# A new order of mixer units and small weights, a fourth product in an accumulator bank, and late low inputs, in a two-layer SSD and DeltaNet trunk

## The chip, the cores and the metric

The kernel runs on one core of one Trainium2 chip. The metric is the device time of one execution in microseconds. The kernel before has a median of 1545.27 us over three runs.

## The reference

The input is one sequence of 256 tokens with 1024 features in float32. Two layers follow, each a half-step SwiGLU feed-forward block, a token mixer and a second feed-forward block. The mixer has a Mamba-2 branch (SSD, 32 heads in four groups) and a gated DeltaNet branch (eight heads) on the same normalised input:

```
for l in range(DEPTH):
    h = h + 0.5 * swiglu(rms_norm(h, ffn1_norm[l]), ffn1_w_in[l], ffn1_w_out[l])
    u = rms_norm(h, mix_norm[l])
    (z_s, xbc, dt_s, qkv, z_d, b_d, a_d, gate_s, gate_d) = jnp.split(u @ w_in[l], split_points, axis=-1)
    y_s = mamba2_branch(z_s, xbc, dt_s, ssm_conv_w[l], ...)
    y_d = deltanet_branch(qkv, z_d, b_d, a_d, dn_conv_w[l], ...)
    merged = (jax.nn.sigmoid(gate_s) * (y_s @ ssm_w_branch[l])
              + jax.nn.sigmoid(gate_d) * (y_d @ dn_w_branch[l]))
    h = h + merged @ w_out[l]
    h = h + 0.5 * swiglu(rms_norm(h, ffn2_norm[l]), ffn2_w_in[l], ffn2_w_out[l])
return rms_norm(h, final_norm)
```

In the Mamba-2 branch, x, B and C go through a causal convolution of four taps and SiLU. Per group and chunk of 128 tokens, the products of C and B are weighted by a decay, applied to x times dt, and joined by the state of the chunk before.

## The kernel before, in words

**Products and weights.** Each float32 product is made of three matmuls: an operand is split into a high part (hi) and the rest (lo), and hi·hi, hi·lo and lo·hi are summed in PSUM. Weights come from HBM as 512 KB forms in one stream on SP's queue into five raw buffers (wraw); ACT writes the high part (whi, L68), DVE the low part (wlo, L71), into five pairs of split buffers. A split pair is rewritten once its last product is done. Activations that enter a product are split in the same way: bh by ACT and bl by DVE for a branch's input, mh and ml for the merged input of the output product.

**PSUM.** Four accumulator banks (`accb`) and four banks for transposes and small products (`trb`) are given out in turn: an allocation gets the bank of the fourth one before it, and its first matmul waits until that tile's last reader is done.

**The mixer's order.** The list ORDER names units, and a scheduler turns the code so written into one instruction stream per engine. The names used here:

- x*gi*: the weights' product for half of group g of x (48 matmuls into an accumulator bank `xs`), then per 128 channels a convolution: one step of ACT and three of DVE (`ca`, of 255, 254 and 253 columns), and SiLU on ACT (`xsT`). The last `ca` steps free the bank.
- D*g*: the decay of group g: a 1 MB DMA of `rdram` into `dc`, then on DVE a subtraction and a minimum with zero, an exponential on ACT, and a product with `cbt` on DVE.
- S*g*: transposes of `xsT` into two banks `xsb`, and on DVE `xD`, `xdt` and `xe` from them.
- T*g*: the products `ydb` (two banks) and `yob`, five sums on DVE, then the sums of squares (`jk`, `sss`), a reciprocal root on POOL (`srr`) and two scalings of `yz` on ACT.
- o: the transposes `oT` of the DeltaNet output's first head pair, `og` on DVE, then its split into bh and bl. y: the same for SSD (`yT`).
- N: the DeltaNet branch's product with its weights, 96 matmuls of 128x512 into four accumulator banks `b` (two halves of the tokens, two of the columns), with the other three `oT` in between.
- g*sni*: a quarter of a gate's product, with `tg` as its result.

Products of C and B (`cbb`, one bank per group, `ssd_pre`) come earlier, at the unit P. Each reads as `cbt` once DVE has masked it. `vb` on DVE is the DeltaNet's last correction, out of a `trb` bank (`ob`).

**The start of a mixer.** Its small weights are loaded on SP: lp (per channel), the next norm's nw, rp (per head, for all rows) and wsr (the 48 columns of dt, b and a), whose high part wsc ACT makes. The small product psm goes through smT and the transposes pst to dt; `ea` and `z` are exponentials on ACT.

**The output product.** `close` calls `out_chunks` for the merged input, k = 0 and 1 first as one group of weights.

Of the kernel before, what the change touches and what calls it, by code (L numbers as in the profile page):

```python
# [7 lines left out]
F32 = mybir.dt.float32  # L8
# [37 lines left out]
ORDER = """  # L46
z20 s z10 z11 s z21 s M k1 k0 q1 k2 k3 K1 K0 q3 q0 K3 K2 v0 q2 I Q0 I Q3 I z30 v1 z31 Q2 v2 V0 I v3
V1 I V3 I Q1 V2 d0 R R R b3 R b2 b0 R b1 R d2 R x00 R d1 x01 R d3 R R P R g100 g101 D0 S0 x10 T0 D1
x11 g110 g111 S1 x20 T1 o x21 N D2 y S2 D3 x30 x31 T2 g000 g010 g001 S3 g011 T3
""".split()  # L50


# [1 line left out]
def trunk_kernel(ctx, tc, x, wst, wsm, norms, lpar, rpar, cst, out):  # L54
# [279 lines left out]
    def mm3(ps, lh, ll, rh, rl, start, stop):  # L334
        PE.matmul(ps, lh, rh, start=start, stop=False)  # L335
        PE.matmul(ps, lh, rl, start=False, stop=False)  # L336
        return PE.matmul(ps, ll, rh, start=False, stop=stop)  # L337
# [55 lines left out]
                        cut and a == 0 and kt == 1,  # L393
                    )

    def out_chunks(ps, stat, ks, last, group=1, split=False, first=None):

        for g0 in range(0, len(ks), group):
            kk = ks[g0 : g0 + group]
            ws = [(k, take()) for k in kk]  # L400
            for t in range(2):
                order = [(k, n) for n in range(2) for k in range(len(kk))]
                if t == 1 and not split:
                    m = len(kk) - 2 if len(kk) == NSPL else len(kk)
                    order = [(k, n) for k in range(m) for n in range(2)]
                    order += [(k, n) for n in range(2) for k in range(m, len(kk))]
                order = [(k, n, 0, 512) for k, n in order]
                if t == 1 and split:
                    order = [o for o in order if o[1] == 0]
                    order += [(k, 1, c, c + 256) for c in (0, 256) for k in range(len(kk))]  # L410
                state["sums"] = []
                for k, n, c0, c1 in order:
                    k, (wh, wl) = ws[k]
                    sh, sl = stat(k, t)
                    c = slice(n * 512 + c0, n * 512 + c1)
                    begin = k == 0 if first is None else first and t == n == 1
                    bank = ps[t][n][:, c0:c1]
                    if c0:
                        begin, bank = k == kk[0], ps[2][:, 0:256]
                    ins = mm3(bank, sh, sl, wh[:, c], wl[:, c], begin, k == last)  # L420
                    state["sums"].append(ins)

    def residual(po, nw):
        def add(t):
# [11 lines left out]

    def close(po, stat, n_k, nw):

        out_chunks(po, stat, list(range(2)), n_k - 1, group=2)
        out_chunks(po, stat, list(range(2, n_k - NSPL)), n_k - 1)  # L440
        state["hold"] = True
        out_chunks(po, stat, list(range(n_k - NSPL, n_k)), n_k - 1, group=NSPL, split=nw is None)
        return residual(po, nw)
# [148 lines left out]

    def mixer(l, nxt):
        with tc.issue_after(state["last"].ins):
            lp = cpool.tile([P, LPW], F32, tag="lp", name="lp")
            nc.sync.dma_start(lp[:], lpar[l])
            rp = cpool.tile([P, RPW], F32, tag="rp", name="rp")
            nc.sync.dma_start(rp[:], rpar[l].partition_broadcast(P))
            wsr = s2.tile([P, KT, 48], F32, tag="s2", name="wsr")
            nc.sync.dma_start(wsr[:], wsm[l])  # L600
        snw = lp[:, 240:256]
        dnw = lp[:, 256:257]
        alog = rp[:, 40:80]
# [47 lines left out]
        def scalars():  # L651
            psm = trb("psm")
            for kt in range(KT):
                both = wsc[:, kt].rearrange("p o c -> p (o c)")
                if kt < KT - 1:
                    PE.matmul(psm[0:96, 0:S], both, uTh[:, kt, :], start=kt == 0, stop=False)
                PE.matmul(psm[0:48, 0:S], wsc[:, kt, 0], uTl[:, kt, :], start=False, stop=False)
                if kt == KT - 1:
                    PE.matmul(psm[0:96, 0:S], both, uTh[:, kt, :], start=False, stop=True)
            smT = s2.tile([96, S], F32, tag="s2", name="smT")  # L660
            act(smT[:], psm[0:96, 0:S])
            pst = trb("pst")
            for t in range(2):
                PE.transpose(pst[:, t * 96 : (t + 1) * 96], smT[:, t * P : (t + 1) * P], ident[0:96, 0:96])
            pv2 = pst[:, 0:192].rearrange("p (t o c) -> p t o c", t=2, o=2)
            pvs = small([P, 2, 48], "pvs", 1)
            pv = pvs[:]
            act(pv, pv2[:, :, 1])
            tt(pv, pv2[:, :, 0], pv, ALU.add)
            scr = s2.tile([P, 5, 2, 40], F32, tag="s2", name="scr")  # L670
            xb, ax, z, s_, q_ = (scr[:, i] for i in range(5))
            tt(xb, pv[:, :, 0:40], rp[:, None, 0:40].to_broadcast([P, 2, 40]), ALU.add)
            act(dq[:, :, 8:16], pv[:, :, 40:48], AF.Tanh, scale=0.5)
            ts(dq[:, :, 8:16], dq[:, :, 8:16], 0.5, ALU.mult, 0.5, ALU.add)
            ea = small([P, 40], "ea", 1)
            with tc.issue_after(state["input"][0].ins):
                act(ea[:], alog, AF.Exp)
            stt(ax, xb, -1.0, xb, ALU.mult, ALU.max)
            act(z, ax, AF.Exp, scale=-1.0)
            ts(s_, z, 2.0, ALU.add)  # L680
            V.reciprocal(out=s_, in_=s_)
            tt(s_, s_, z, ALU.mult)
            tt(q_, s_, s_, ALU.mult)
            ts(z, q_, 1.0 / 15.0, ALU.mult)
            for d_ in (13.0, 11.0, 9.0, 7.0, 5.0, 3.0):
                stt(z, z, 1.0 / d_, q_, ALU.add, ALU.mult)
            stt(z, z, 1.0, s_, ALU.add, ALU.mult)
            ts(ax, xb, 0.0, ALU.max)
            stt(sp[:], z, 2.0, ax, ALU.mult, ALU.add)
            stt(la[:], sp[:], -1.0, ea[:, None, :].to_broadcast([P, 2, 40]), ALU.mult, ALU.mult)  # L690
            yield
            psr = trb("psr")
            for t in range(2):
                PE.matmul(psr[0:40, t * 256 : (t + 1) * 256], la[:, t, :], UU, start=True, stop=True)
            pr = psr[:].rearrange("p (t c) -> p t c", t=2)
            V.tensor_copy(rows[0:32], pr[0:32, :, 0:P])
            V.tensor_copy(rows[32:40], pr[32:40, :, P : 2 * P])
            nc.sync.dma_start(rdram[:], rows[:].rearrange("p t c -> p (t c)"))
            pac = trb("pac")
            for t in range(2):  # L700
                PE.transpose(pac[:, t * 40 : (t + 1) * 40], rows[:, t, :], ident[0:40, 0:40])
            V.tensor_copy(ac[:], pac[:, 0:80].rearrange("p (t c) -> p t c", t=2))
            V.tensor_copy(dq[:, :, 0:8], ac[:, :, 32:40])
            yield
            psp = trb("psp")
            for c in range(4):
                PE.matmul(psp[:, c * 16 : (c + 1) * 16], SEL[c % 2], dq[:, c // 2, :], start=True, stop=True)
            for a in range(2):
                V.tensor_copy(
                    pq[64 * a : 64 * a + 64].rearrange("p k h c -> p c k h"),  # L710
                    psp[64 * a : 64 * a + 64, 0:64].rearrange("p (c k h a) -> p c k h a", c=4, k=2, h=4)[:, :, :, :, a],
                )
# [325 lines left out]
        def ssd_pre():  # L1038
            BT, CT = late["BC"][:, 0:4], late["BC"][:, 4:8]
            cbt = slots.tile([P, 3 * GS, P], F32, tag="sF", name="cbt")  # L1040
            late["cbx"] = cbx = cbt[:, 2 * GS :]
            late["cbm"] = cbm = cbt[:, : 2 * GS].rearrange("p (g t) l -> p g t l", g=GS)
            for g in range(GS):
                cbb = trb("cbb")
                PE.matmul(cbb[:, 0 : 2 * P], BT[:, g, 0:P], CT[:, g, :], start=True, stop=True)
                PE.matmul(cbb[:, 2 * P : 3 * P], BT[:, g, P : 2 * P], CT[:, g, P : 2 * P], start=True, stop=True)
                tt(
                    cbm[:, g],
                    cbb[:].rearrange("p (t o l) -> p t o l", t=2, o=2)[:, :, 0, :],
                    U[:, None, :].to_broadcast([P, 2, P]),  # L1050
                    ALU.mult,
                )
                act(cbx[:, g], cbb[:, P : 2 * P])
            yield
# [226 lines left out]
    norm_first(nw0)  # L1281
    for l in range(DEPTH):
        ffn(norm_vec(3 * l + 1))
        mixer(l, norm_vec(3 * l + 2))
        add = ffn(norm_vec(3 * l + 3) if l + 1 < DEPTH else None)
    nw = norm_vec(3 * DEPTH)
    for t in range(2):
# [151 lines left out]
```

## Time and profile before

| | us |
|---|---|
| median of three runs | 1545.27 (1545.19 to 1546.01) |
| the profiled execution, its own time | 1543.84 |
| its span, first to last instruction | 1542.1 |
| PE busy | 1525.1 |
| DVE busy | 1229.8 |
| ACT busy | 949.8 |
| POOL busy | 82.6 |

PE is TensorE, DVE VectorE, ACT ScalarE, POOL GpSimd, SP SyncE. A row of the timeline gives a start, a busy time, the engine, the line, the operation with output and inputs, the shape and the count, and in brackets the idle time ahead of it with what ended it. Successive instructions overlap by a little, so the time that one costs in a queue is read from start to start. The list of waits gives for each line and releaser the total in us, the number and the longest. A window gives for a stretch of time the busy us of PE, of PE's weight loads, DVE, ACT and POOL, each with its count, then the granted clock, the DMA share and GB/s.

### The profile page before, as it was taken

The page shows a single profiled execution, that of the slowest core. Times are in us where ns is not written, and L with a number is a line of the kernel's source. Part 1 is how long each engine was busy: PE and PEld are TensorE (multiplying, and loading weights), DVE is VectorE, ACT ScalarE, POOL GpSimd, SP SyncE. Part 2 cuts the span into 40 slices and gives each one's busy share as a digit, 9 for nine tenths or more (in the row PEclk, how much of TensorE's full clock was granted, in tenths as well). Part 3 has the DMA queues.
Part 4 walks back from the last instruction along what each step waited for, and adds up shares of the span by engine and source line. Part 5 has one row for each costly group of instructions (what it writes and reads, how often), then busy time and mean ns, then how long its engine had stood idle before and what let it go on. Part 6 is the DMA issues. An engine that isn't in the chain of part 4 may idle for free.

```text
span 1542.1 us, 29082 instructions
## 1 busy us (share of the span) xinstructions
PE 1525.1 (99%) x11473; PEld 1385.3 (90%) x11473; DVE 1229.8 (80%) x1859; ACT 949.8 (62%) x1536; POOL 82.6 (5%) x92
## 2 busy tenths in 40 slices
PE   8999999999999999999999999999999999999998
PEld 7999879999988888999899998899998888899997
DVE  5878768967899766789778887689579996678886
ACT  5656667766665645566555566776756666455565
POOL 0000010000000000000100012010000000000010
PEclk9999999999999999999999999999999999999999
DMA  7687765553565556577866687566346555556775
GB/s 272 187 266 227 232 223 174 183 164 112 180 209 172 157 174 191 184 252 217 264 221 227 204 254 238 182 196 186 117 137 204 180 167 187 175 179 191 250 241 156
DMA packets 98831, 305.73 MB, mean 198 GB/s; under 512 B 22837, under 2 KB 23813, under 8 KB 97670
## 3 DMA queue, kind: packets, MB, share of 16 engines
q1 hardware_dynamic: 93796, 290.95, 57.1%
q0 software_dynamic: 4608, 12.58, 5.0%
q8 instruction: 90, 1.47, 0.4%
q14 instruction: 47, 0.39, 0.1%
q10 hardware_dynamic: 290, 0.33, 0.1%
HBM read 297.72 MB, written 1.92 MB: 194 GB/s over the span
## 4 chain that ended last, share of the span: by engine, by line
PE 90%; DVE 3%; ACT 3%; DMA 2%; issue 1%; POOL 0%; SPq 0%; POOLq 0%; ACTq 0%; DVEq 0%
PE fc L346 10%; PE fc L340 9%; PE fc L345 9%; PE t L366 9%; PE o L337 4%; PE o L336 4%; PE o L335 4%; PE f L366 3%; PE b L337 3%; PE b L335 3%; PE b L336 3%; PE p L336 2%; PE p L335 2%; PE p L337 2%; PE xs L340 1%; PE xs L345 1%
## 5 line engine op out<-in xcount | busy, mean ns | idle before, releaser
L71 DVE TENSOR_TENSOR wlo<-wraw,whi 128x1024 fp32r<-128x1024 f32 x488 | 592.2, 1222 | 189.9 <-ACT whi L68 175.4
L68 ACT ACTIVATE whi<-wraw 128x1024 fp32r<-128x1024 f32 x488 | 511.4, 1059 | 266.8 <-PE fc L345 87.3
L346 PE MATMUL fc<-uW,wlo 128*128 128x256 f32 x1280 | 354.9, 277 | 0.0
L340 PE MATMUL fc<-uW,whi 128*128 128x256 f32 x1280 | 354.1, 277 | 0.0
L345 PE MATMUL fc<-uW,whi 128*128 128x256 f32 x1260 | 348.3, 276 | 0.0
L340 PEld LDWEIGHTS fc<-uW,whi 128*128 128x128 f32 x1280 | 240.5, 188 | 0.8
L346 PEld LDWEIGHTS fc<-uW,wlo 128*128 128x128 f32 x1280 | 240.5, 188 | 0.0
L345 PEld LDWEIGHTS fc<-uW,whi 128*128 128x128 f32 x1260 | 236.5, 188 | 0.8
L366 PE MATMUL t<-whi,uW 128*128 128x512 f32 x512 | 165.4, 397 | 0.0
L366 PEld LDWEIGHTS t<-whi,uW 128*128 128x128 f32 x512 | 95.9, 188 | 21.6 <-issue 1.3
L68 ACT ACTIVATE whi<-wsum 128x1024 fp32r<-128x1024 f32 x64 | 68.0, 1062 | 58.7 <-PE fc L345 32.3
L366 PE MATMUL t<-wlo,uW 128*128 128x512 f32 x256 | 100.1, 392 | 0.0
L71 DVE TENSOR_TENSOR wlo<-wsum,whi 128x1024 fp32r<-128x1024 f32 x64 | 78.2, 1222 | 8.3 <-ACT whi L68 5.9
L335 PE MATMUL b<-whi,bh 128*128 128x512 f32 x192 | 76.1, 398 | 0.3 <-ACT bh L68 0.2
L336 PE MATMUL b<-wlo,bh 128*128 128x512 f32 x192 | 75.0, 390 | 0.0
L337 PE MATMUL b<-whi,bl 128*128 128x512 f32 x192 | 74.3, 394 | 0.3 <-DVE bl L71 0.3
L340 PE MATMUL xs<-uW,whi 128*128 128x256 f32 x256 | 72.8, 284 | 0.0
L346 PE MATMUL xs<-uW,wlo 128*128 128x256 f32 x256 | 71.4, 279 | 0.0
L345 PE MATMUL xs<-uW,whi 128*128 128x256 f32 x254 | 70.5, 278 | 0.0
L335 PE MATMUL o<-whi,gh 128*128 128x512 f32 (+1 forms) x160 | 62.0, 388 | 0.0
L337 PE MATMUL o<-whi,gl 128*128 128x512 f32 (+1 forms) x160 | 61.8, 386 | 0.0
L336 PE MATMUL o<-wlo,gh 128*128 128x512 f32 (+1 forms) x160 | 61.7, 386 | 0.0
(337 smaller groups left out, 3301.2 us busy)
## 6 DMA issues: line engine op xcount, KB each, us to landing
wraw<-in_wst_dram SPq DMA_DIRECT2D x504, 512.0 KB, 4.8
wsum<-in_wst_dram SPq DMA_DIRECT2D x16, 512.0 KB, 7.3
wsum<-in_wst_dram POOLq DMA_DIRECT2D x16, 512.0 KB, 8.6
dc<-rdram SPq DMA_DIRECT2D x8, 1024.0 KB, 8.6
nw<-in_norms_dram SPq DMA_DIRECT2D x6, 512.0 KB, 5.3
h<-u POOLq DMA_DIRECT2D x12, 256.0 KB, 6.4
gb<-rdram SPq DMA_DIRECT2D x8, 256.0 KB, 6.1
h<-in_x_dram SPq DMA_DIRECT2D x4, 256.0 KB, 3.7
```

What stands on the lines that cost most here:

```text
L68: return A.activation(out=o, in_=i, func=func, **kw)
L71: return V.tensor_tensor(out=o, in0=a, in1=b, op=op)
L335: PE.matmul(ps, lh, rh, start=start, stop=False)
L336: PE.matmul(ps, lh, rl, start=False, stop=False)
L337: return PE.matmul(ps, ll, rh, start=False, stop=stop)
L340: PE.matmul(ps, wh, mh, start=start, stop=False)
L345: PE.matmul(ps, wh, ml, start=False, stop=False)
L346: PE.matmul(ps, wl, mh, start=False, stop=stop)
L366: ins = PE.matmul(ps[t][:], st, mv, start=k0 == 0 and j == 0, stop=k0 == KT - 2 and j == 5)
```

## The change

Five edits:

1. In ORDER, x20 comes ahead of S1, and T1 behind x21.
2. In the output product's first group, for the first half of the tokens, the products with the input's low part come after all those with its high part (`defer`).
3. At the start of a mixer wsr is loaded first, then rp and lp, and the next norm's nw after them; wsr lies in the slot y3 and not in the pool s2.
4. `ea`'s exponential comes behind that of `z`.
5. The last of the four products of C and B goes to an accumulator bank.

```
-x11 g110 g111 S1 x20 T1 o x21 N D2 y S2 D3 x30 x31 T2 g000 g010 g001 S3 g011 T3
+x11 g110 g111 x20 S1 o x21 T1 N D2 y S2 D3 x30 x31 T2 g000 g010 g001 S3 g011 T3
...
-    def out_chunks(ps, stat, ks, last, group=1, split=False, first=None):
+    def out_chunks(ps, stat, ks, last, group=1, split=False, first=None, defer=False):
...
-                state["sums"] = []
+                state["sums"], lows = [], []
...
+                    if defer and t == 0:
+                        PE.matmul(bank, sh, wh[:, c], start=begin, stop=False)
+                        PE.matmul(bank, sh, wl[:, c], start=False, stop=False)
+                        lows.append((bank, sl, wh[:, c]))
+                        continue
                     ins = mm3(bank, sh, sl, wh[:, c], wl[:, c], begin, k == last)
                     state["sums"].append(ins)
+                for bank, sl, high in lows:
+                    PE.matmul(bank, sl, high, start=False, stop=False)
...
-        out_chunks(po, stat, list(range(2)), n_k - 1, group=2)
+        out_chunks(po, stat, list(range(2)), n_k - 1, group=2, defer=True)
...
+            wsr = slots.tile([P, KT, 48], F32, tag="y3", name="wsr")
+            nc.sync.dma_start(wsr[:], wsm[l])
+            rp = cpool.tile([P, RPW], F32, tag="rp", name="rp")
+            nc.sync.dma_start(rp[:], rpar[l].partition_broadcast(P))
             lp = cpool.tile([P, LPW], F32, tag="lp", name="lp")
             nc.sync.dma_start(lp[:], lpar[l])
-            rp = cpool.tile([P, RPW], F32, tag="rp", name="rp")
-            nc.sync.dma_start(rp[:], rpar[l].partition_broadcast(P))
-            wsr = s2.tile([P, KT, 48], F32, tag="s2", name="wsr")
-            nc.sync.dma_start(wsr[:], wsm[l])
+        nxt = norm_vec(nxt)
...
-            with tc.issue_after(state["input"][0].ins):
+            stt(ax, xb, -1.0, xb, ALU.mult, ALU.max)
+            with tc.issue_after(act(z, ax, AF.Exp, scale=-1.0).ins):
                 act(ea[:], alog, AF.Exp)
-            stt(ax, xb, -1.0, xb, ALU.mult, ALU.max)
-            act(z, ax, AF.Exp, scale=-1.0)
...
-                cbb = trb("cbb")
+                cbb = trb("cbb") if g < GS - 1 else accb("cbb")
...
-        mixer(l, norm_vec(3 * l + 2))
+        mixer(l, 3 * l + 2)
```

The number of matmuls stays; ACT has four instructions fewer, all of them table loads.

PE at the product N of layer 0, before: b_5569 to b_5572 are its four banks, whi and bh its weights' and its input's high parts, bh_5492 the first head pair and bh_5627 the third.

```order
L335 MATMUL b_5569<-whi_5586,bh_5627 128x512
L336 MATMUL b_5569<-wlo_5587,bh_5627 128x512
L335 MATMUL b_5570<-whi_5586,bh_5627 128x512
L336 MATMUL b_5570<-wlo_5587,bh_5627 128x512
L335 MATMUL b_5571<-whi_5586,bh_5627 128x512
L336 MATMUL b_5571<-wlo_5587,bh_5627 128x512
L1169 MATMUL yT_5760<-cs_79,yz_2179 128x128
L337 MATMUL b_5569<-whi_5586,bl_5628 128x512
L337 MATMUL b_5570<-whi_5586,bl_5628 128x512
L335 MATMUL b_5572<-whi_5361,bh_5492 128x512
L336 MATMUL b_5572<-wlo_5362,bh_5492 128x512
```

There the fourth bank, b_5572, got its first product after the other three had begun with the third head pair. The same place now, where the first head pair is bh_5439 and bh_5580 the second:

```order
L1161 MATMUL oT_5620<-cs_79,vb_2285 128x2x64 x4
L1161 MATMUL oT_5667<-cs_79,vb_2285 128x2x64 x4
L1176 MATMUL yT_5760<-cs_79,yz_2179 128x128 x4
L335 MATMUL b_5572<-whi_5341,bh_5439 128x512
L336 MATMUL b_5572<-wlo_5342,bh_5439 128x512
L337 MATMUL b_5572<-whi_5341,bl_5440 128x512
L335 MATMUL b_5572<-whi_5347,bh_5439 128x512
L336 MATMUL b_5572<-wlo_5348,bh_5439 128x512
L337 MATMUL b_5572<-whi_5347,bl_5440 128x512
L1108 MATMUL xsb_5771<-cs_79,xsT_5337 128x128 x4
L335 MATMUL b_5569<-whi_5446,bh_5580 128x512
L336 MATMUL b_5569<-wlo_5447,bh_5580 128x512
```

All four banks now take the first head pair before any takes the second, and transposes of the next group (xsb_5771) stand between.

DVE at the same place, before: ca_5426 is x20's convolution, ca_5557 that of x21, og_5578 and bl_5581 belong to the second head pair, sss to T1.

```order
L74 SCALAR_TENSOR_TENSOR ca_5426<-xs_5358,lp_2173,ca_5426 128x253
L79 TENSOR_SCALAR sss_5473<-sss_5473 128x2
L71 TENSOR_TENSOR wlo_5506<-wraw_5305,whi_5505 128x1024
L71 TENSOR_TENSOR bl_5493<-og_5490,bh_5492 128x512
L74 SCALAR_TENSOR_TENSOR ca_5557<-xs_5496,lp_2173,ca_5557 128x255
L74 SCALAR_TENSOR_TENSOR og_5578<-oT_5573,lp_2173,zdT_4029 128x512
L74 SCALAR_TENSOR_TENSOR ca_5557<-xs_5496,lp_2173,ca_5557 128x254
```

T1's sums ended ahead of x21's convolution, and og_5578 stood within it. Now, with ca_5510 the second half of x21's convolution:

```order
L71 TENSOR_TENSOR xD_5426<-xD_5426,yo_5554 128x512
L74 SCALAR_TENSOR_TENSOR ca_5510<-xs_5443,lp_2175,ca_5510 128x254
L71 TENSOR_TENSOR yz_2398<-yz_2398,xD_5417 128x512
L74 SCALAR_TENSOR_TENSOR ca_5510<-xs_5443,lp_2175,ca_5510 128x253
L71 TENSOR_TENSOR yz_2398<-yz_2398,xD_5426 128x512
L71 TENSOR_TENSOR wlo_5587<-wraw_5339,whi_5586 128x1024
L79 TENSOR_SCALAR sss_5557<-sss_5557 128x2
L74 SCALAR_TENSOR_TENSOR og_5578<-oT_5573,lp_2175,zdT_4029 128x512
L71 TENSOR_TENSOR wlo_5593<-wraw_5345,whi_5592 128x1024
L71 TENSOR_TENSOR dc_5791<-dc_5791,ac_2267 128x2048
L71 TENSOR_TENSOR bl_5581<-og_5578,bh_5580 128x512
```

T1's sums and both halves of x21's convolution now run into one another, and og_5578 and bl_5581 stand behind both. On ACT the split of that og follows T1's two scalings:

```order
L68 ACTIVATE jk_5562,sss_5557<-yz_2398 128x512
L68 ACTIVATE whi_5592<-wraw_5345 128x1024
L68 ACTIVATE yz_2398<-yz_2398,srr_5565 128x512 x2
L68 ACTIVATE bh_5580<-og_5578 128x512
L68 ACTIVATE whi_5633<-wraw_5444 128x1024
```

Before, a weight's split (whi_5586) stood between the scalings and bh_5580, with the scalings further ahead of og_5578.

## The prediction

> **What bounds the kernel now.** I read the page's busy times first, then the waits of PE, then the busy time in the stretch that the new order touches.
>
> ```profile
> span 1542.1 us, 29082 instructions
> PE 1525.1 (99%) x11473; PEld 1385.3 (90%) x11473; DVE 1229.8 (80%) x1859; ACT 949.8 (62%) x1536; POOL 82.6 (5%) x92
> ```
>
> PE is busy 1525.1 of 1542.1 us. The change leaves the number of matmuls as it is, so it can only move PE's waits. The view of PE's waits (total us, times, longest) has those that the change touches:
>
> ```profile
> PE xsb L1101 <- ACT xsT L68: 1.7, 2, 0.9
> PE cbb L1045 <- DVE vb L71: 1.3, 2, 0.9
> PE o L337 <- DVE ml L71: 0.6, 2, 0.3
> PE pst L664 <- ACT smT L68: 0.5, 1, 0.5
> PE b L337 <- DVE bl L71: 0.3, 1, 0.3
> PE b L335 <- ACT bh L68: 0.2, 1, 0.2
> ```
>
> Together they are 4.6 us in two layers: that is about all there is to win. Measured from start to start they are a little larger:
>
> ```profile
> 444.83 0.28 PE L345 MATMUL xs<-uW,whi 128*128 128x256 f32 x1
> 446.04 0.44 PE L1101 MATMUL xsb<-cs,xsT 128*128 128x128 f32 x2 [0.93 <-ACT xsT L68]
> ```
>
> Here 1.21 us pass where neighbouring xs matmuls are 0.12 apart (48 of them in 5.5 us, by two rows further down), so 1.1 is lost where the row says 0.93: each wait costs about 0.2 more than its row.
>
> What the new order may collide with shows in the windows from S1 to the end of N (busy us of PE, PEld, DVE, ACT, POOL), in layer 0:
>
> ```profile
> 442.00:485.00 43.00, 41.58 (x301) 35.71 (x300) 41.01 (x54) 26.80 (x37) 2.21 (x1) 1.00 0.53 170
> ```
>
> DVE is 80% busy over the span, but 41.0 of 43 us here. Whoever asks DVE for something earlier in this stretch will wait for it.
>
> **The change part by part.** *The order of units.* Before, S1's transposes (xsb) came ahead of x20 and waited for x11's convolution; T1 lay between x20 and x21. Now it is x20, S1, oT0, x21, T1, N: PE no longer waits for xsT, but both convolutions of x20 and x21 and all of T1 come to DVE closer ahead of N. N needs four accumulator banks, and its last one, b_5572, is the bank that x21's convolution reads. Before, that bank's first product stood behind the third pair of weight forms and yT; now it is the 19th product of N.
>
> I replay layer 0 from these rows, first PE's:
>
> ```profile
> 442.56 0.82 PE L1101 MATMUL xsb<-cs,xsT 128*128 128x128 f32 x6
> 450.29 2.08 PE L1115 MATMUL ydb<-xdt,dc 128*64 128x64 f32 x64
> 453.26 0.60 PE L1154 MATMUL oT<-cs,vb 128*128 128x128 f32 x4
> 453.62 0.37 PE L340 MATMUL xs<-uW,whi 128*128 128x256 f32 x1
> 459.16 1.25 PE L1154 MATMUL oT<-cs,vb 128*128 128x128 f32 x10
> 461.15 0.40 PE L335 MATMUL b<-whi,bh 128*128 128x512 f32 x1
> 461.38 0.39 PE L336 MATMUL b<-wlo,bh 128*128 128x512 f32 x1
> ```
>
> An x unit takes 5.5 (453.62 to 459.16), T1's ydb and yob 3.0 (450.29 to 453.26), a set of four transposes 0.4, a product of N 0.23. From 442.56, where g11 ends: x20 to 448.2, S1's xsb to 449.2, oT0 to 449.65, x21 to 455.1, T1 to 458.0, oT1 and the first 18 products to 462.7, oT2, oT3 and yT to 464.0. There PE wants b_5572. Now DVE:
>
> ```profile
> 445.00 0.48 DVE L74 SCALAR_TENSOR_TENSOR ca<-xs,lp,ca 128x253 f32<-128x253 f32 x1
> 445.39 1.22 DVE L71 TENSOR_TENSOR wlo<-wraw,whi 128x1024 fp32r<-128x1024 f32 x1
> 446.52 0.69 DVE L71 TENSOR_TENSOR xD<-xsb,rp 128x512 f32<-128x512 f32 x1
> 447.12 0.68 DVE L71 TENSOR_TENSOR xdt<-xsb,sp 128x512 f32<-128x512 f32 x1
> 449.51 1.22 DVE L78 TENSOR_SCALAR dc<-dc 128x2048 f32<-128x2048 f32 x1
> 461.88 0.75 DVE L74 SCALAR_TENSOR_TENSOR og<-oT,lp,zdT 128x512 f32<-128x512 f32 x1
> 462.54 0.48 DVE L74 SCALAR_TENSOR_TENSOR ca<-xs,lp,ca 128x254 f32<-128x254 f32 x1
> 467.67 2.28 DVE L71 TENSOR_TENSOR dc<-dc,cbt 128x2048 f32<-128x2048 f32 x1
> 469.86 0.48 DVE L74 SCALAR_TENSOR_TENSOR ca<-xs,lp,ca 128x254 f32<-128x254 f32 x1
> ```
>
> Start to start, a wlo takes 1.13, the decay's tensor-scalar with the same busy time as much, a 128x512 product 0.60, a convolution step 0.40, an og 0.65, a dc product 2.2. Up to 445.4 DVE's order is the old one. From there to x21's last convolution step it has four wlo (4.5), a tensor-scalar (1.1), ten 128x512 products (6.0), a bl (0.6), an og (0.65), a dc product (2.2) and twelve convolution steps (4.8): 19.9, and about 0.3 of idle time behind ACT. So b_5572 comes free at 465.7 and PE has waited **1.8**. Its six products end at 467.3; then come the transposes xsb_5771, into the bank that og_5578 reads. DVE has a yz, a wlo and the sums of T1 (sss) ahead of og: 467.5 to 468.25. PE waits **1.0**, and reaches the products with bh_5580 at 468.75. That bh is made by ACT, in its order behind both yz of T1, which wait for POOL's reciprocal root of sss:
>
> ```profile
> 459.92 2.21 POOL L210 TENSOR_TENSOR srr<-sss,mhalf 128x2 f32<-128x2 f32 x1 [25.59 <-DVE sss L79]
> 1222.41 1.61 POOL L210 TENSOR_TENSOR srr<-sss,mhalf 128x2 f32<-128x2 f32 x1 [25.77 <-DVE sss L79]
> 462.16 1.34 ACT L68 ACTIVATE yz<-yz,srr 128x512 f32<-128x512 f32 x2 [1.32 <-POOL srr L210]
> 464.35 0.61 ACT L68 ACTIVATE bh<-og 128x512 fp32r<-128x512 f32 x1
> 451.81 1.28 ACT L68 ACT_TABLE_LOAD   x1
> ```
>
> sss ends at 467.5; 2.21, 1.34 and 0.6 with the handovers put bh at 471.75: PE waits **3.0**. bl_5581 stands on DVE behind og, a wlo and a dc product of D3, to about 472.5, and PE asks for it eight products later, at 473.6. New waits in layer 0: 5.8; in layer 1, where POOL took 1.61, 5.2. Old ones that go: xsb, bl and bh of N, 2.2 by the rows, and 3.1 with 0.2 for each and a bh in layer 1 too short for the list. Of this part, 11.0 − 3.1 = **+7.9**.
>
> *The other edits.* The fourth cbb no longer waits for the bank that vb frees behind a dc product; the deferral puts six other products (1.4 us) between ml and its first use; pst waits for smT, which two table loads and a late wsr pushed back. By the rows 1.3 + 0.6 + 0.5 = 2.4, with 0.2 for each of five waits 3.4; I take **−2.9**.
>
> *Costed at nothing.* The small weights:
>
> ```profile
> 192.88 0.42 SPq L596 DMA_DIRECT2D lp<-in_lpar_dram  x1
> 195.68 0.38 SPq L600 DMA_DIRECT2D wsr<-in_wsm_dram  x1
> 201.84 0.53 ACT L68 ACTIVATE wsc<-wsr 128x384 fp32r<-128x384 f32 x1 [2.42 <-DMA wsr<-in_wsm_dram]
> ```
>
> wsr took 6.1 us to land; issued first, where lp stood (192.9), it lands near 199, so ACT's queue (yz and a whi behind wsc) stands less than before. nw, now last of the four, still has its weight forms to land in, and slot y3's next tenant is written after wsc has read wsr. Of the five split buffers four are ahead of the next whi, each good for 12 products of 0.23 us: 11 us cover ACT here; without that cover its lateness would be PE's, us for us. Two table loads fewer per layer are 2.6 us of ACT, which is 62% busy, so nothing on PE beyond pst. The accumulator bank that cbb takes was read long before. D3's transfer waits on SP until T1's ydb have been read, and the weight form behind it with it:
>
> ```profile
> dc<-rdram SPq DMA_DIRECT2D x8, 1024.0 KB, 8.6
> ```
>
> Issued about 457, behind ydb in the replay, it lands at 466, ahead of DVE's dc product, which og and a wlo put at 469.4; without that margin bl_5581 would be late by as much.
>
> Sum: +7.9 − 2.9 = **+5.0**. On the profiled execution (1543.84 us, 1542.1 its span) that is 1548.8; the median of the runs, 1545.27, is 1.43 above this execution, and so the forecast is 1550.3.
>
> Bounds of the main case: if the wlo ahead of sss falls into one of DVE's gaps, all behind it comes 1.1 earlier in each layer, and with savings of 3.4 the sum is 5.0 − 2.2 − 0.5 = +2.3, 1547.6. If ACT puts a table load of 1.28 ahead of bh in each layer, and the savings are 2.4, it is 5.0 + 2.6 + 0.5 = +8.1, 1553.4.
>
> **The rivals.** *A, faster.* DVE runs ahead by as much as it is late in my replay (5.8 us), so that no new wait comes. For it: DVE idles 20% of the span, and the replay may charge it for work that fits into its gaps. Against it: 41.0 of 43 us, with wlo paced by ACT and the released weight buffers. Then only savings are left: −3.1 − 2.9 = −6.0, 1539.3.
>
> *B, no change.* DVE is about 2 us ahead of the replay, and the waits come to 3.4 per layer, most of it bh's. 6.8 − 3.1 − 2.9 = +0.8, 1546.0.
>
> *C, slower by more.* The three waits come within 8 us and the granted clock drops behind them. The trace shows half rate at the program's start:
>
> ```profile
> 10.70 1.75 PE L366 MATMUL f<-whi,uW 128*128 128x512 f32 x3
> 12.24 1.48 PE L366 MATMUL f<-wlo,uW 128*128 128x512 f32 x3
> 13.52 1.91 PE L366 MATMUL f<-whi,uW 128*128 128x512 f32 x4
> 15.23 0.69 PE L282 MATMUL hnT<-cs,hn 128*128 128x128 f32 x4
> ```
>
> Ten matmuls in 4.53 us, 0.45 each against 0.23 later: 2.25 lost. Once in each layer, +4.5, 1554.8. Against it: 0.93 us of waiting at 446.04 left the pace of the xs matmuls at 0.12, and the window shows clock 1.00. [...]
>
> **How the numbers follow.** This kernel's runs spread by 0.05%; about 0.2% (3.1 us) can be told from no change, so the bounds are 1542.2 and 1548.4. Main case 0.67, of which 0.10 lies under 1548.4; A 0.20, B 0.08, C 0.05. Faster 0.20; same 0.08 + 0.10 = 0.18; slower 0.57 + 0.05 = 0.62. The main case's own range is 1547.6 to 1553.4. The range, 1540.0 to 1555.0, takes in B, the bounds of the main case and C, and reaches into A, leaving out about 0.12 of it.
>
> **What would show it.** In the profile after, the waits for xsT, vb, ml and smT are gone; new ones stand at b L335 within 460 to 475 (for DVE's convolution step, then for ACT bh, of about 3 us), at L1101 for og, and the same in layer 1 around 1222 to 1238. On ACT, bh follows right behind yz<-yz,srr. The forecast is wrong if b_5572 starts without a wait, since then DVE had slack that the windows hide (A or B), and it is wrong in its size if bh comes well before or after yz. If xs or b matmuls run at 0.4 us behind the waits, it is C.

## The result, and the profile after

The changed kernel took 1550.01 us (median of seven runs, 1547.96 to 1553.34), the kernel before 1545.19 (seven runs, 1544.36 to 1547.49). The ratio is 1.0031, with a 95% interval of 1.0020 to 1.0042: 3.1 to 6.5 us slower, 4.8 by the ratio. The profiled execution is one of the longer ones: 1552.75 us, 2.7 above the median.

From the page, as before:

```profile
span 1551.0 us, 29084 instructions
PE 1528.9 (99%) x11473; PEld 1387.5 (89%) x11473; DVE 1230.3 (79%) x1859; ACT 944.3 (61%) x1532; POOL 81.9 (5%) x92
```

PE's waits, those at N and one more:

```profile
PE b L335 <- DVE ca L74: 5.0, 4, 1.8
PE b L335 <- ACT bh L68: 2.2, 2, 1.4
PE xs L346 <- DVE wlo L71: 1.3, 1, 1.3
PE xsb L1108 <- DVE og L74: 0.8, 1, 0.8
```

Five of the six waits that the prediction listed are gone, 4.4 us by the rows; the sixth, for bh at N, is 2.2 instead of 0.2. N now waits for x20's and x21's convolution (ca), for og and for bh: 8.0 us by the rows. A wait for a wlo, far ahead of N, is new too. The places in layer 0, from PE's timeline, with the releaser in the brackets:

```profile
461.66 0.47 PE L335 MATMUL b<-whi,bh 128*128 128x512 f32 x1 [0.68 <-DVE ca L74]
...
466.61 0.47 PE L335 MATMUL b<-whi,bh 128*128 128x512 f32 x1 [1.80 <-DVE ca L74]
...
468.98 0.66 PE L1108 MATMUL xsb<-cs,xsT 128*128 128x128 f32 x4 [0.77 <-DVE og L74]
...
470.99 0.50 PE L335 MATMUL b<-whi,bh 128*128 128x512 f32 x1 [1.35 <-ACT bh L68]
```

The releasers, from the timelines of DVE, POOL and ACT:

```profile
465.99 0.47 DVE L74 SCALAR_TENSOR_TENSOR ca<-xs,lp,ca 128x253 f32<-128x253 f32 x1
...
468.11 0.16 DVE L79 TENSOR_SCALAR sss<-sss 128x2 f32<-128x2 f32 x1
468.18 0.74 DVE L74 SCALAR_TENSOR_TENSOR og<-oT,lp,zdT 128x512 f32<-128x512 f32 x1
468.86 1.22 DVE L71 TENSOR_TENSOR wlo<-wraw,whi 128x1024 fp32r<-128x1024 f32 x1
```

```profile
468.35 0.69 POOL L210 TENSOR_TENSOR srr<-sss,mhalf 128x2 f32<-128x2 f32 x1 [31.30 <-DVE sss L79]
```

```profile
469.08 1.33 ACT L68 ACTIVATE yz<-yz,srr 128x512 f32<-128x512 f32 x2 [0.26 <-POOL srr L210]
470.32 0.61 ACT L68 ACTIVATE bh<-og 128x512 fp32r<-128x512 f32 x1
```

The last step of x21's convolution ends at 466.46 and PE starts on b_5572 at 466.61; og ends at 468.92 and the transposes start at 468.98; bh follows right behind the scalings of yz, and PE starts on it at 470.99. Windows of layer 1 (busy us of PE, PEld, DVE, ACT, POOL, then the granted clock) show one thing more:

```profile
1225.00:1230.00 5.00, 4.32 (x23) 3.27 (x22) 5.00 (x10) 2.13 (x4) 0.00 (x0) 1.00 0.89 339
1230.00:1235.00 5.00, 3.17 (x14) 1.84 (x11) 5.00 (x10) 2.71 (x7) 0.50 (x1) 0.85 0.02 8
1235.00:1238.00 3.00, 1.98 (x6) 1.49 (x7) 3.00 (x3) 2.77 (x4) 0.19 (x1) 0.50 0.61 195
1238.00:1240.00 2.00, 2.00 (x6) 1.51 (x6) 2.00 (x4) 0.30 (x2) 0.00 (x0) 0.50 0.61 193
1240.00:1242.00 2.00, 2.00 (x10) 1.59 (x9) 2.00 (x3) 0.36 (x1) 0.00 (x0) 0.91 0.23 57
```

The clock fell to one half, while PE went through these waits, and came back at about 1240.3. PE's rows there:

```profile
1237.13 0.79 PE L335 MATMUL b<-whi,bh 128*128 128x512 f32 x1 [0.89 <-ACT bh L68]
...
1238.15 0.63 PE L335 MATMUL b<-whi,bh 128*128 128x512 f32 x1
1238.58 0.63 PE L336 MATMUL b<-wlo,bh 128*128 128x512 f32 x1
...
1240.56 0.39 PE L337 MATMUL b<-whi,bl 128*128 128x512 f32 x1
1240.79 0.40 PE L335 MATMUL b<-whi,bh 128*128 128x512 f32 x1
```

A product takes 0.43 instead of 0.23, and the eight from 1237.13 to 1240.56 take 3.43 instead of 1.82: 1.6 us lost. What ran slower before 1237.13 cost nothing, since PE then waited for bh anyway.

How the loss divides over the two layers is read from PE's transposes hnT, which open a mixer and the feed-forward block behind it. They start at 186.84 and 596.43 in layer 0 and at 951.41 and 1363.97 in layer 1; before, at 186.70, 593.34, 948.28 and 1355.23. So layer 0, where the clock stayed at 1.00, took 3.0 us longer, and layer 1 5.6, with the 1.6 of the clock and the 1.3 of the wlo in it.

### The profile page after: what moved, and what is told of

The parts are those of the page before. It is cut to its first block, busy times and chain, and to the rows that moved or that the text cites. A ratio compares the mean times of both kernels' runs of the same rounds, so it can differ in the third digit from the quotient of the medians.

```text
span 1551.0 us, 29084 instructions
## 1 busy us (share of the span) xinstructions
PE 1528.9 (99%) x11473; PEld 1387.5 (89%) x11473; DVE 1230.3 (79%) x1859; ACT 944.3 (61%) x1532; POOL 81.9 (5%) x92
## 4 chain that ended last, share of the span: by engine, by line
PE 88%; DVE 6%; ACT 2%; DMA 2%; issue 1%; SPq 1%; POOL 0%; POOLq 0%; DVEq 0%; ACTq 0%
PE fc L346 9%; PE fc L340 9%; PE t L366 9%; PE fc L345 9%; PE o L336 4%; PE o L335 4%; PE o L337 4%; PE f L366 3%; PE b L335 3%; PE b L336 3%; PE b L337 3%; PE p L336 2%; PE p L337 2%; PE p L335 2%; PE xs L346 2%; PE xs L340 2%
```

## The experiments

Each kernel was timed in five rounds beside the kernel before, in three groups. The kernel before itself had medians of 1545.69, 1545.09 and 1543.62 in them (the third on another chip), so what follows compares the ratios; 0.001 is 1.5 us. Edits are shown against the changed kernel; the new order alone, and x20 first without the other edits, are shown against the kernel before.

### The old order with the other four edits

```
-x11 g110 g111 x20 S1 o x21 T1 N ...
+x11 g110 g111 S1 x20 T1 o x21 N ...
```

> The changed kernel with the old ORDER (S1 x20 T1 o x21 N); the other four edits stay. Theory (the loss is all in the new order, through convolution steps, og and bh that DVE and ACT deliver late to N): the waits for ca, og and bh in N are gone, those for xsT are back (about 2.0 in two layers), and what is left is the saving of the other edits, 3.4 us by the two traces: 1541.8; if the new wait of 1.3 us at xs for a wlo in layer 1 belongs to the other edits, 1543.2. Rival (one of the other edits costs time, the order little): 1547 or more, with the waits at N mostly gone.

Measured: 1545.33 us, ratio 0.9995 (0.9986 to 1.0004). The loss is gone with the order, as the theory said, but the other edits win 0.8 us, not 3.4. Waits and PE's timeline at S1 show a part of why:

```profile
PE xsb L1108 <- ACT xsT L68: 3.7, 2, 2.1
```

```profile
444.86 0.44 PE L1108 MATMUL xsb<-cs,xsT 128*128 128x128 f32 x2 [1.58 <-ACT xsT L68]
...
1206.26 0.44 PE L1108 MATMUL xsb<-cs,xsT 128*128 128x128 f32 x2 [2.09 <-ACT xsT L68]
```

The wait for xsT was 1.7 in the kernel before and is 3.7 here: in layer 0 PE comes to S1 1.8 us earlier, but xsT only 1.2. Two of the 3.4 us are given back there. The traced execution is the fastest of the eleven, 3.5 us below their median, and its clock was 0.999; the mean granted clock of all eleven is 0.9979, against 0.9989 of the kernel before beside it. So the clock may have taken a part of the saving too, but the trace does not show it.

### The new order alone

```
-x11 g110 g111 S1 x20 T1 o x21 N ...
+x11 g110 g111 x20 S1 o x21 T1 N ...
```

> The kernel before with the new ORDER alone. Theory: the waits at N as in the changed kernel, +4.1 and +4.5 us in the two layers as its trace has them without the dip of the clock, none of the savings: 1553.8, and up to 1557 where the granted clock drops behind the waits. Rival (the loss comes from the other edits): within 2 us of 1545.2.

Measured: 1550.07 us, ratio 1.0025 (1.0016 to 1.0035), 3.9 us. The rival is out; the theory's size (8.6) is over twice what was measured. Its waits at N:

```profile
PE b L335 <- ACT bh L68: 2.7, 2, 1.4
PE xsb L1101 <- DVE og L74: 2.6, 2, 1.3
```

There is none for ca. PE comes to N later here, since it still waits for vb and smT ahead of it: in layer 0 N's first product starts at 460.48 instead of 457.99. And DVE is done with x21's convolution sooner, at 465.73 instead of 466.46: D2's product with cbt, 2.28 us long, stands behind og (at 469.89), where the changed kernel has it ahead of that convolution (at 456.54). The theory took the waits over from the changed kernel's trace, and with them DVE's order there.

### x20 first, T1 in its old place

```
-x11 g110 g111 x20 S1 o x21 T1 N ...
+x11 g110 g111 x20 S1 T1 o x21 N ...
```

> The changed kernel with x20 ahead of S1 but T1 back before x21 (x20 S1 T1 o x21 N). Theory (T1 behind x21 is what makes DVE late for N): the waits for xsT stay gone and those for ca, og and bh go too, so about 2 us less than the kernel with the old order: 1540 to 1541.5. Rival (x20 ahead of S1 does it, since all of S1's work on DVE comes 6 us later): the waits at N stay, about 1549.

Measured: 1540.25 us, ratio 0.9960 (0.9948 to 0.9973): the fastest of all, faster than both kernels. The theory holds: no wait at N in its list. One new wait, at S1's own products:

```profile
PE ydb L1122 <- DVE xdt L71: 1.6, 2, 1.1
```

### S1 in its old place, T1 late

```
-x11 g110 g111 x20 S1 o x21 T1 N ...
+x11 g110 g111 S1 x20 o x21 T1 N ...
```

> The changed kernel with S1 ahead of x20 as before and T1 behind x21 (S1 x20 o x21 T1 N). Theory (T1 behind x21 is the cause): waits for ca, og and bh at N within 1 us a layer of those of the changed kernel, and the waits for xsT (2.0) besides: 1550 to 1552. Rival (x20 ahead of S1 is the cause): no waits at N, 1542 to 1543.

Measured: 1550.16 us, ratio 1.0027 (1.0015 to 1.0039), the time the theory gave. T1 behind x21 costs the time, not x20 ahead of S1. The waits differ in kind from the forecast: 5.1 us are at S1, and those at N come to 4.9, where the changed kernel has 8.0; ca is not among them.

```profile
PE xsb L1108 <- ACT xsT L68: 5.1, 2, 2.5
...
PE b L335 <- ACT bh L68: 2.4, 2, 1.2
...
PE xsb L1108 <- DVE og L74: 1.8, 2, 0.9
PE b L337 <- DVE bl L71: 0.7, 2, 0.3
```

### The changed kernel with 2.2 us less on DVE per layer

```
+            if g != 1:
                 tt(dc[:], dc[:], late["cbm"][:, g, None].to_broadcast([P, 8, 2, P]), ALU.mult)
```

> The changed kernel without one DVE instruction per layer: the decay of group 1 is not multiplied by the product of C and B (2.2 us of DVE, between S1 and x20's convolution; this leaves out part of the computation). Theory (N waits for the end of DVE's queue: convolution of x21, sums of T1, og): the waits at N, 5.3 and 4.9 us in the two layers, shrink by 2 each, and with fewer dips of the clock the time falls by 4 to 6: 1544 to 1546. Rival (N waits for POOL's root and ACT behind it, or for banks, whatever DVE has to do): less than 1 us, 1549 to 1550.

Measured: 1542.97 us, ratio 0.9985 (0.9976 to 0.9993); against the 1.0031 of the changed kernel that is 7 us less, with an interval of about 2 to either side, and more than the theory's 4 to 6. The product left out is D1's; in the changed kernel it stands at 430.11, ahead of S1 and not behind it as the expectation has it, and D2's moves up without it, from 456.54 to 443.73. One DVE instruction of 2.2 us per layer off the queue took away more than it lasted, since PE then no longer waits for og and bh:

```profile
PE b L335 <- DVE ca L74: 3.9, 2, 1.9
```

That is all that is left at N. DVE's queue set the end; the rival (POOL, ACT or banks whatever DVE does) is out.

### The old order, and the old bank

```
-x11 g110 g111 x20 S1 o x21 T1 N ...
+x11 g110 g111 S1 x20 T1 o x21 N ...
...
-                cbb = trb("cbb") if g < GS - 1 else accb("cbb")
+                cbb = trb("cbb")
```

> The kernel with the old order and the other four edits, now with the fourth product of C and B back in the bank that vb frees. Theory (what the bank edit saves, 1.8 us in two layers, is given back at S1, where xsT then waits 3.7 instead of 1.7): the waits for vb return (1.3 to 1.9), those for xsT fall to about 1.7 to 2, and the time stays within 1 us of the kernel with the bank edit. Rival (the savings add up): 1.8 us more, 1547.

Measured: 1542.98 us, ratio 0.9986 (0.9977 to 0.9996). The rival is out: without the bank edit the kernel is 1.4 us faster, with an interval of about 2 to either side. That is a little beyond the 1 us that the theory allowed, but within the noise, so a loss by the bank edit is not shown. The waits changed places as the theory has it, by more than it said (this traced execution is the slowest of the eleven):

```profile
PE cbb L1052 <- DVE vb L71: 3.0, 2, 1.8
...
PE xsb L1108 <- ACT xsT L68: 0.9, 1, 0.9
```

### x20 first, T1 in its old place, none of the other edits

```
-x11 g110 g111 S1 x20 T1 o x21 N ...
+x11 g110 g111 x20 S1 T1 o x21 N ...
```

> The kernel before with x20 ahead of S1 and T1 before x21, nothing else. Theory (the order alone takes away the wait for xsT, 2.0 in two layers, and lets the other edits' savings through, which the old order gave back): 1543 to 1543.7, so that of the 5.4 us of this order with all edits 3 to 3.4 belong to the other edits. Rival (this order alone is worth all 5): 1540 to 1541.

Measured: 1546.02 us, ratio 1.0006 (0.9997 to 1.0015). Both missed: alone the order wins nothing, and with the other edits it wins 6.2. The wait for xsT is gone, but N has another:

```profile
PE b L335 <- ACT bh L68: 2.3, 2, 1.2
```

POOL and DVE ahead of that bh:

```profile
460.13 3.34 POOL L210 TENSOR_TENSOR srr<-sss,mhalf 128x2 f32<-128x2 f32 x1 [25.59 <-DVE sss L79]
```

```profile
459.96 1.22 DVE L71 TENSOR_TENSOR wlo<-wraw,whi 128x1024 fp32r<-128x1024 f32 x1
461.10 0.68 DVE L71 TENSOR_TENSOR bl<-og,bh 128x512 fp32r<-128x512 f32 x1
461.70 1.22 DVE L71 TENSOR_TENSOR wlo<-wraw,whi 128x1024 fp32r<-128x1024 f32 x1
462.84 0.47 DVE L74 SCALAR_TENSOR_TENSOR ca<-xs,lp,ca 128x255 f32<-128x255 f32 x1
```

Three tensor-tensor operations stand behind sss here, and POOL's root ended 0.63 after the last of them gave way (462.84 to 463.47). The same three, in the same order, stand behind sss in the kernel with x20 first and all other edits. But there POOL's root was done much sooner:

```profile
458.86 1.60 POOL L210 TENSOR_TENSOR srr<-sss,mhalf 128x2 f32<-128x2 f32 x1 [23.01 <-DVE sss L79]
```

It ended 0.63 after the first of the three gave way to bl (459.83 to 460.46), and N has no wait for bh in that kernel. The last section comes back to this.

### x20 first, T1 in its old place, with the old bank

```
-x11 g110 g111 x20 S1 o x21 T1 N ...
+x11 g110 g111 x20 S1 T1 o x21 N ...
...
-                cbb = trb("cbb") if g < GS - 1 else accb("cbb")
+                cbb = trb("cbb")
```

> The order x20 S1 T1 o x21 N with all other edits but the bank of the fourth product of C and B, which is the old one. Theory (where nothing behind it waits for DVE, the bank edit's saving comes through): the waits for vb are back (1.3 to 2.0 by the rows), and the time is 1.5 to 2.5 us above the same kernel with the bank edit: 1541.8 to 1542.8. Rival (the bank edit is worth nothing or costs time, as the old order seemed to show): 1539 to 1540.5.

Measured: 1542.80 us, ratio 0.9998 (0.9989 to 1.0006). Against the same kernel with the bank edit (0.9960) that is 5.9 us more, with about 2.3 to either side: the theory's direction, over twice its size. Here N has the wait of the kernel above again, and POOL's root takes 3.34 again, where the same kernel with the bank edit has 1.60 behind the same operations of DVE. So a part of the 5.9 goes with POOL's longer root and not with the wait that the bank edit takes away. By the rows of the two traces the difference is 2.1 (2.3 for bh and 1.4 for vb here, 1.6 for xdt there); the rest is not accounted for.

```profile
PE b L335 <- ACT bh L68: 2.3, 2, 1.2
```

### The changed kernel with the old bank

```
-                cbb = trb("cbb") if g < GS - 1 else accb("cbb")
+                cbb = trb("cbb")
```

> The changed kernel with the old bank for the fourth product of C and B. Theory (DVE's queue sets the end of N in the new order, so that what PE gains ahead of it is given back there): the waits for vb return, those for ca at N shrink by as much, and the time stays within 1 us of the changed kernel, 1549 to 1551. Rival (the bank edit saves its 1.8 us in this order too): 1551.8.

Measured: 1546.99 us, ratio 1.0020 (1.0011 to 1.0029). It lies 1.7 us below the changed kernel, with about 2.2 to either side, so the rival (1.8 above) is out. Waits for vb are back (1.1), those for ca have gone, and og and bh stay:

```profile
PE b L335 <- ACT bh L68: 2.7, 2, 1.4
...
PE xsb L1108 <- DVE og L74: 2.6, 2, 1.3
```

The time is within noise of the theory's 1 us, but the waits are not what it said: those for ca shrink by more than the 1.1 of vb. As with the new order alone, D2's product stands behind og on DVE (at 467.89), and in layer 0 x21's convolution ends at 463.73, 0.16 before PE starts on its bank.

## Why the prediction was right, and where it was not

**The total and its cause.** Forecast +5.0, measured +4.8. The cause is the one named: in the new order N asks for x21's bank, og and bh before DVE and ACT have them. It was shown by the old order (the loss goes), by T1 alone moved back (it goes too, and more) and by 2.2 us less on DVE (7 us less).

**The replay.** In layer 0 it had b_5572 free at 465.7, og read at 468.25 and bh ready at 471.75; PE went on at 466.6, 469.0 and 471.0. The three waits were to be 1.8, 1.0 and 3.0; by the rows they are 1.80, 0.77 and 1.35, and there is a fourth, 0.68 for x20's bank, which the replay left out. The first two hold. For layer 1 it had 5.2 in all; the rows there have 0.68, 1.81 and 0.89, and none for og.

**The third wait was mis-sized.** It took POOL's root at the 2.21 of the profile before (1.61 in layer 1). It takes 0.69 and 0.70 after, where og stands behind sss on DVE and not a wlo. The order that the prediction drew on shows og there; the price did not look at it.

**The other edits were mis-sized.** Their −2.9 was to come on top. With the old order they bring −0.8 (−2.2 to +0.6), and −2.2 without the bank edit (−3.6 to −0.6). The waits that they take away are gone, as the prediction said, but it did not ask what is late next: xsT, whose wait grew by 2.0. The order's +7.9 is +3.9 alone (2.5 to 5.4), and on top of the new order the other edits bring nothing that can be told: 1.0031 with them and 1.0025 without, 0.9 us more with about 2.2 to either side. Both terms were too large, and that the sum fits is partly luck: they are not independent. What PE gains ahead of N can become a longer wait there.

**Rival C came true in part.** It was to happen once in each layer at 2.25, on top of the main case. In the profiled execution the clock dipped in layer 1 alone, and 1.6 us of it reached the end. (The half rate at the program's start, from which the prediction took its price, shows in the rows only; the window view has a granted clock of 1.00 from 10 to 15 there.) The mean clock of the seven runs is 0.9971, and the times spread by 5.4 us; the two with 0.995 took 1551.11 and 1553.34. The main case had no such term, so a part of the +4.8 comes from a rival that was given 0.05, by the author's estimate. How large that part is at the median was not measured.

**Costed at nothing.** No wait for wsc, smT or the D3 transfer shows in the list of waits, so these cost nothing. But a transfer on SP's queue did cost time, one that the prediction did not look at. The wait of 1.3 for a wlo ahead of x10, in layer 1, goes back to D0's transfer into dc: it was issued at 1160.32 and took 10.08 us to land, DVE sat idle for it for 2.63 us, and everything behind it on DVE came later, to the wlo that PE waited for until 1184.69. In the kernel with T1 late D0's transfer took 9.58 in layer 0, and PE waited 0.6 for a wlo there. In the other kernels no landing that DVE waited for took more than 9.11, and they have no such wait. Why the transfer takes longer at times stays open.

## What to carry to other kernels

Where PE is busy 99% of the time, look for the engine that is full in the same window (DVE, busy for 41.0 of 43 us around N before the change) before moving work there: when a unit moves closer to its consumer, the time that this engine lacks becomes a wait, here 8.0 us by the rows. Savings in front of such a place are not added; follow each to the next wait. An order should be tried again after every other edit: x20 first with T1 left alone gained 6 us, but only with the bank edit, and the bank edit gained nothing in the two other orders. Part of that hung on one POOL instruction, which took 1.60 us in one kernel and 3.34 in the other behind the same operations of DVE: compare such rows before an order gets the credit.

## What the runs showed of the hardware

**POOL's root took longer behind tensor-tensor operations of DVE.** `srr`, 128x2 elements, took 0.69 to 3.34 us. In the changed kernel it took 0.69 and 0.70 where og stood behind sss; in the kernel before 1.60 behind one wlo and 2.21 behind wlo and bl; in the kernel with x20 first alone 3.34 behind wlo, bl and wlo. In these two kernels it ended 0.63 or 0.64 after the last of them gave way to the next instruction, and in the case of 3.34 its record lasts through all three. In the kernel with T1 late it took 3.27. The runs show the times and the order of the rows, not what POOL does in between.

Three roots are exceptions: that of T1 in layer 1 of the kernel before (1.61 with wlo and bl behind sss) and those of T1 in both layers of x20 first with all other edits (1.60 with wlo, bl and wlo). They ended 0.63 or 0.64 after the first wlo gave way to bl. ACT's bh, which bl reads, had ended 0.24 us before bl began in the first of the three, and 0.27 in layer 0 of the other kernel. Beside roots that took 2.21 and 3.34 it was 0.35 (layer 0 of the kernel before) and 0.56 (layer 0 of x20 first alone). Whether this decides the root's time no run tests.

**The clock fell behind a wait of 1.8, in one layer of two.** In layer 1 of the changed kernel it fell to 0.50 about 1 us behind a wait of 1.81 that ended at 1232.75, which had one of 0.68 some 5 us ahead of it, and stayed down for some 6.5 us. PE was busy for 3.17 us in the window from 1230 to 1235. In layer 0 of the same execution waits of 0.68 and 1.80, and two more of 0.77 and 1.35, left it at 1.00, though PE was busy for only 2.26 of the 5 us from 465 to 470. Why one layer dipped and the other did not, the runs do not show. Over the runs, kernels whose longest wait after the program's start was 1.2 or less in their one trace had a mean clock of 0.9989 to 0.9991 (before, x20 first with and without the other edits or the bank), those with waits of 1.8 to 2.5 had 0.9971 to 0.9979, save the one with the old order and old bank (1.8 in its profile, 0.9989); the new order alone and with the old bank had 0.9974 and 0.9977 at pairs of 1.3 to 1.4 within two us.
